# Two FFNs in fp32: four of eight k-tile pairs by seven products, two pairs with parts made by DMAs, and x accumulated in DRAM

## The chip, the core and the metric

The kernel runs on one core of a Trainium2 chip. The metric is the device time of the whole program in microseconds (us). Engines are named as the profile names them: PE is the matmul engine and PEld its weight loads, DVE the vector engine, ACT the scalar engine, POOL the GpSimd engine, SP the engine that issues most of the DMAs.

## The reference

The program is one fp32 forward pass of 256 tokens at width 2048 through two layers. Each layer is a mixer (a state-space scan beside sparse attention in the first; block attention beside a gated delta rule in the second) and an FFN with squared ReLU. The change concerns the two FFNs alone:

```python
# first layer, 256 tokens; w_up is 2048 x 8192, w_down 8192 x 2048
u = rmsnorm(x, g_mlp) @ w_up
return x + jnp.square(jax.nn.relu(u)) @ w_down
# second layer
return x + jnp.square(jax.nn.relu(h @ w_up)) @ w_down
```

## The kernel before

**Parts.** An fp32 value is split into a high part, the value rounded to the matmul format fp32r, and a low part, the value minus its high part. A product of fp32 operands is three matmuls: high by high, high of the activations by low of the weights, low of the activations by high of the weights (`product`, L250). Weights come from DRAM as fp32 in tiles `wst`, one SP DMA of 1024 KB each; ACT copies 1024 columns into a `whi` tile (L266) and DVE subtracts it into a `wlo` tile (L267). `stp` holds 3 tiles `wst`, `whp` and `wlp` 4 tiles each.

**A wide.** `wide` (L240) multiplies 256 tokens by a block of 2048 x 1024 weights. It goes through eight pairs j of two k-tiles (256 rows of weights) and accumulates in four of the eight PSUM banks at a time, and in four more for the parts of the seven products. For an ordinary pair each of two k-tiles meets two token tiles and two column halves: eight products, 24 matmuls of 128x512, in two ACT copies and two DVE subtractions. For j in `SPAIRS` = (2, 4, 6) the pair is treated as a 2 x 2 block product in seven products, 21 matmuls. DVE first makes four block differences of the weights (`t13` at L284, `t24` at L287 and L288), and the sums of the activation blocks stand ready in `forms[j]` (`two_forms`, `a_forms`). `shared` (L308) adds the PSUM banks together at the end, in four tiles of [128, 512].

**An FFN.** `ffn` (L374) has four stages `s_`, each with two wides of `w_up` and two of `w_down`; the last wide of `w_down` is done as two `panel`s instead. That makes 15 wides in one FFN and 30 in the program. I number them n = 0 to 14 in each FFN: n = 0, 1, 4, 5, 8, 9, 12, 13 are up wides and the rest down wides. Behind an up wide come squared ReLU (L382, L383) and 16 transposes on PE (L395), whose results are split into `hTh` and `hTl` (four k-tiles, two pairs, in each), and for pairs in `SPAIRS` are copied to `ff` (L399) and formed into `sfh` and `sfl`. Behind a down wide DVE adds the result to x, which lies in SBUF in four tiles X[p] of [128, 2, 512], in two additions for each quarter (L415, L418).

**Order and storage.** Each engine runs its instructions in the order that the tile scheduler has written down. Tiles come from pools with a fixed number of slots, and a tile waits for its slot until the last use of the tile that had it. The pool `sp` has 7 slots of 4 KB per partition. During an FFN four of these hold X, and the other three serve `t13` and `t24`. `ff` lies in the larger pool `s4`.

**POOL** has next to nothing to do: 51 rows in the program, among them the reciprocal roots of L159, and it issues no DMA in the FFNs.

Of the kernel before, what the change touches and what calls it, by code (L numbers as in the profile page):

```python
# [57 lines left out]
def build(ctx, tc, I, out, tap=None, upto=99):  # L58
    nc = tc.nc
# [179 lines left out]

    def wide(w, r0, c0, lhs, forms):  # L240

# [21 lines left out]
        def parts(src, n=1024):  # L263
            a = whp.tile([128, 1024], F32R, name="whi")
            b = wlp.tile([128, 1024], F32R, name="wlo")
            S.activation(a[:, :n], src, AF.Copy)  # L266
            V.tensor_tensor(b[:, :n], src, a[:, :n].bitcast(F32), op=OP.subtract)  # L267
            return [(a[:, o:o + 512], b[:, o:o + 512]) for o in range(0, n, 512)]

        for j in range(8):  # L270
            s = stp.tile([128, 2048], F32, name="wst")
            nc.sync.dma_start(s.rearrange("p (k n) -> p k n", k=2),
                              w[r0 + j * 256:r0 + j * 256 + 256, c0:c0 + 1024].rearrange("(k p) n -> p k n", p=128))
            if j not in SPAIRS:
                for kk in range(2):
                    xh, xl = lhs(2 * j + kk)
                    wl = parts(s[:, kk * 1024:(kk + 1) * 1024])[::-1]
                    for i, l, b in ((0, 0, "P2"), (0, 1, "P3"), (1, 0, "P4"), (1, 1, "E")):
                        h = slice(i * 128, i * 128 + 128)
                        product(b, xh[:, h], xl[:, h], *wl[l])  # L280
                continue
# [18 lines left out]
            product("P7", *sums(3), *u3)  # L300
            u2, u4 = parts(flat(t24))
            product("P6", *sums(2), *u2)
# [5 lines left out]
    def shared(B):  # L308

        p1, u2, u4, v = (s2([128, 512], name=n) for n in ("cp1", "cu2", "cu4", "cv"))  # L310
        S.activation(p1, B["P1"], AF.Copy)
        V.tensor_tensor(u2, B["P6"], p1, op=OP.add)
        V.tensor_tensor(u4, B["P5"], u2, op=OP.add)
        V.tensor_tensor(u2, B["P7"], u2, op=OP.add)
        V.tensor_tensor(v, B["P5"], u2, op=OP.add)
        return ((0, 0, p1, B["P2"]), (0, 1, u4, B["P3"]), (1, 0, u2, B["P4"]), (1, 1, v, B["E"]))

# [53 lines left out]
    def flat(ap):  # L371
        return ap.rearrange("p k c -> p (k c)")

    def ffn(X, act, forms, w_up, w_down, r, after, tail=0):  # L374
        for s_ in range(4):
            hT, hforms = [], {}
            for P in range(2):
                B, tags = wide(w_up, 0, s_ * 2048 + P * 1024, at_k(act), forms)
                us = {}
                for i, l, part, bank in shared(B):  # L380
                    V.tensor_tensor(part, bank, part, op=OP.add)
                    S.activation(part, part, AF.Relu, scale=r[:, i:i + 1])  # L382
                    S.activation(part, part, AF.Square)  # L383
                    us[i, l] = part
                for l in (1, 0):
# [3 lines left out]
                    for k0 in range(0, 4, 2):  # L389
# [11 lines left out]
                        else:  # L401
                            split(pt, flat(q[0][:, k0:k0 + 2]), flat(q[1][:, k0:k0 + 2]))
            for P in range(2):
                if (s_, P) == (3, 1):
                    for p in (2, 3):
# [4 lines left out]
                    continue  # L410
                B, _ = wide(w_down, s_ * 2048, P * 1024, at_k(hT), hforms)
                out_ = shared(B)
# [6 lines left out]
                if s_ == 3:  # L419
                    for p in range(2):  # L420
                        for t in range(2):
                            after(p, t)
# [367 lines left out]
    def add_panel(ps, p, scale, act, gain, ssx, forms):  # L790
# [601 lines left out]
```

## Time and profile before

| | us |
|---|---|
| three runs | 2635.05, 2633.22, 2637.54 |
| median | 2635.05 |
| the profiled execution, its own time | 2632.15 |
| its span | 2630.4 |
| first FFN in the trace, from its first to its last wide | 381.7 to 1102.6 |
| second FFN in the trace, with the end of the program | 1934.0 to 2621.6 |

The profiled execution is 2.9 us below the median, and its span leaves out 1.75 us at its ends. In the page, part 1 gives each engine's busy time as a share of the span, part 2 draws that over 40 slices of 66 us with the granted clock of PE, and part 6 gives the median time from issue to landing of each kind of DMA. A view by stretches gives busy times, the number of instructions in brackets, the granted clock, the DMA engines' mean share and the GB/s moved. A view of waits names who waits for whom, how long in total and how often. The timeline lists instructions by start and duration. PE's matmuls overlap each other, so the distance between two starts is what one of them takes of PE's time, and not its duration.

### The profile page before, as it was taken

What the parts mean: (1) busy time and instruction counts of PE and PEld (TensorE: products, weight loads), DVE (VectorE), ACT (ScalarE), POOL (GpSimd) and SP (SyncE); (2) the same over time, 40 slices, a digit from 0 to 9 for tenths busy, and PEclk for the clock granted to TensorE, in tenths of its full rate; (3) what the DMA queues carried; (4) which work ended last, traced back from release to release, by engine and by line L of the source; (5) the groups of instructions that cost most, each with busy time, mean ns of one, the idle gap of its engine ahead of it and who ended that gap; (6) DMA issues with size and microseconds to landing.
All of it is one profiled execution on the core that took longest, in us unless ns stands there. A gap on an engine that the chain in (4) does not pass through costs nothing.

```text
span 2630.4 us, 32664 instructions
## 1 busy us (share of the span) xinstructions
PE 2602.5 (99%) x12566; PEld 2171.2 (83%) x12566; DVE 2033.5 (77%) x2791; ACT 1463.4 (56%) x1956; POOL 38.6 (1%) x46
## 2 busy tenths in 40 slices
PE   8999999999999999999999999999999999999998
PEld 8998888878888888888888887888888888888886
DVE  5767768999989999676754767455579999999996
ACT  5455456646657566554533555444457566566664
POOL 0000000000000000000100000000000000000000
PEclk9999999999999999999999999999999999999999
DMA  7454555565555656653432743556555655565655
GB/s 239 142 176 157 168 192 192 179 205 192 192 201 183 208 194 199 210 186 119 133 96 87 252 166 112 180 189 211 198 180 178 215 199 195 193 207 191 208 179 173
DMA packets 192154, 478.64 MB, mean 182 GB/s; under 512 B 9127, under 2 KB 50046, under 8 KB 191998
## 3 DMA queue, kind: packets, MB, share of 16 engines
q1 hardware_dynamic: 185840, 467.57, 53.6%
q10 hardware_dynamic: 6158, 8.99, 1.0%
q8 instruction: 98, 1.61, 0.2%
q14 instruction: 58, 0.48, 0.1%
HBM read 472.32 MB, written 4.21 MB: 181 GB/s over the span
## 4 chain that ended last, share of the span: by engine, by line
PE 90%; DVE 5%; DMA 2%; ACT 1%; issue 1%; ACTq 0%; POOL 0%; POOLq 0%; SPq 0%; DVEq 0%
PE mm L255 21%; PE mm L193 13%; PE mm L194 13%; PE mm L192 13%; PE tp L255 10%; PE sx L255 9%; DVE wlo L267 3%; DMA wst<-in_w_down_dram 1%; PE sx L987 1%; PE sx L982 1%; PE tp L350 1%; ACT whi L266 1%; PE mm L395 1%; PE tp L881 0%; DVE wlo L208 0%
## 5 line engine op out<-in xcount | busy, mean ns | idle before, releaser
L208 DVE TENSOR_TENSOR wlo<-wst,whi 128x1024 fp32r<-128x1024 f32 (+6 forms) x416 | 475.7, 1146 | 319.8 <-ACT whi L207 316.8
L207 ACT ACTIVATE whi<-wst 128x1024 fp32r<-128x1024 f32 (+6 forms) x416 | 414.4, 998 | 461.7 <-PE mm L194 432.9
L266 ACT ACTIVATE whi<-wst 128x1024 fp32r<-128x1024 f32 x480 | 465.8, 979 | 275.8 <-PE mm L255 116.0
L267 DVE TENSOR_TENSOR wlo<-wst,whi 128x1024 fp32r<-128x1024 f32 x480 | 527.9, 1119 | 58.5 <-ACT whi L266 55.9
L266 ACT ACTIVATE whi<-t 128x1024 fp32r<-128x1024 f32 x180 | 190.2, 1057 | 214.2 <-DVE t L288 89.2
L193 PE MATMUL mm<-wlo,x2h 128*128 128x512 f32 (+3 forms) x736 | 279.1, 379 | 1.5 <-DVE wlo L208 1.5
L194 PE MATMUL mm<-whi,x2l 128*128 128x512 f32 (+3 forms) x736 | 279.2, 379 | 0.0
L192 PE MATMUL mm<-whi,x2h 128*128 128x512 f32 (+3 forms) x736 | 279.0, 379 | 0.0
L267 DVE TENSOR_TENSOR wlo<-t,whi 128x1024 fp32r<-128x1024 f32 x180 | 219.6, 1220 | 41.3 <-ACT whi L266 39.4
L193 PEld LDWEIGHTS mm<-wlo,x2h 128*128 128x128 f32 x736 | 138.9, 189 | 22.0 <-DVE wlo L208 2.1
L192 PEld LDWEIGHTS mm<-whi,x2h 128*128 128x128 f32 x736 | 138.9, 189 | 20.3 <-issue 1.1
L194 PEld LDWEIGHTS mm<-whi,x2l 128*128 128x128 f32 x736 | 138.6, 188 | 20.0 <-issue 0.9
L192 PE MATMUL mm<-whi,xnh 128*128 128x512 f32 (+3 forms) x416 | 152.6, 368 | 2.0 <-ACT whi L207 1.6
L255 PE MATMUL mm<-wlo,xnh 128*128 128x512 f32 x392 | 153.0, 390 | 0.0
L255 PE MATMUL mm<-whi,xnl 128*128 128x512 f32 x392 | 152.7, 390 | 0.0
L255 PE MATMUL mm<-whi,xnh 128*128 128x512 f32 x392 | 151.9, 391 | 0.7 <-ACT whi L266 0.7
L193 PE MATMUL mm<-wlo,xnh 128*128 128x512 f32 (+3 forms) x416 | 152.0, 366 | 0.0
L194 PE MATMUL mm<-whi,xnl 128*128 128x512 f32 (+3 forms) x416 | 150.7, 365 | 0.0
L255 PE MATMUL mm<-wlo,hTh 128*128 128x512 f32 x343 | 133.9, 390 | 0.0
L255 PE MATMUL mm<-whi,hTl 128*128 128x512 f32 x343 | 133.6, 389 | 0.0
L255 PE MATMUL mm<-whi,hTh 128*128 128x512 f32 x343 | 132.0, 390 | 0.0
L284 DVE TENSOR_TENSOR t<-wst 128x1024 f32<-128x1024 f32 x90 | 109.7, 1219 | 13.4 <-DMA wst<-in_w_down_dram 10.9
(531 smaller groups left out, 5407.9 us busy)
## 6 DMA issues: line engine op xcount, KB each, us to landing
wst<-in_w_up_dram SPq DMA_DIRECT2D x128, 1024.0 KB, 5.0
wst<-in_w_down_dram SPq DMA_DIRECT2D x128, 1024.0 KB, 5.4
wst<-in_w_in_dram SPq DMA_DIRECT2D x84, 1024.0 KB, 5.1
wst<-in_w_out_dram SPq DMA_DIRECT2D x16, 1024.0 KB, 5.1
wst<-in_w_o_dram SPq DMA_DIRECT2D x16, 1024.0 KB, 5.0
wst<-in_w_in_dram SPq DMA_DIRECT2D x16, 780.0 KB, 4.4
wst<-in_w_in_dram SPq DMA_DIRECT2D x12, 824.0 KB, 4.6
wst<-in_w_in_dram SPq DMA_DIRECT2D x12, 736.0 KB, 6.3
```

Of the source, the lines that this page charges most:

```text
L192: PE.matmul(ps[t][:, :n], xh[:, sl], wa, start=kt == first, stop=False)
L193: PE.matmul(ps[t][:, :n], xh[:, sl], wb, start=False, stop=False)
L194: PE.matmul(ps[t][:, :n], xl[:, sl], wa, start=False, stop=kt == last)
L207: S.activation(a[:, :2 * n], src, AF.Copy)
L208: V.tensor_tensor(b[:, :2 * n], src, a[:, :2 * n].bitcast(F32), op=OP.subtract)
L255: PE.matmul(B[b], x, y, start=left[b] == total[b], stop=left[b] == 1)
L266: S.activation(a[:, :n], src, AF.Copy)
L267: V.tensor_tensor(b[:, :n], src, a[:, :n].bitcast(F32), op=OP.subtract)
L284: V.tensor_tensor(t13, s.rearrange("p (k l n) -> p k l n", k=2, l=2)[:, :, 0], s[:, :1024].rearrange("p (l n) -> p l n", l=2)[:, ::-1], op ...
L350: PE.transpose(ps[:, kk, t, :], x[:, t, (k0 + kk) * 128:(k0 + kk + 1) * 128], ident)
L395: PE.transpose(pv[:, kk, t, :], us[t, l][:, c:c + 128], ident)
L982: PE.matmul(ps[:, i * 64:(i + 1) * 64].rearrange("p (m b) -> p m b", b=b), N[:, i], half(T[:, i], 0), start=True, stop=True)
```

## The change

- `SPAIRS` is (2, 3, 5, 6): four pairs of each wide go by seven products instead of three.
- Pair 4 of wides n = 0 to 13, and pair 0 of wides n = 1 to 13, are ordinary and their weights don't come through `wst`. `far_load` makes their parts: a GpSimd DMA of 512 KB from DRAM into an fp32r tile `fhi` rounds them; ACT writes the negative of `fhi` into `flo`; a second GpSimd DMA of the same weights is accumulated onto `flo`. That leaves `flo` = weights minus their high part. No DVE instruction is needed. Each pair takes four such DMAs, two rounding and two accumulating, so that 27 pairs make 108 DMAs in each FFN.
- Pair 4 of a wide is asked for when the code comes to pair 1 of the same wide, and pair 0 of the next wide when it comes to pair 5 (`hooks`).
- `fhi` and `flo` lie in the pool `sp`. X leaves it: x is stored to a DRAM tensor `xd` ahead of the FFN (ACT's queue), the results of the down wides of the first three stages are added to `xd` by accumulating GpSimd DMAs of 512 KB (12 in each FFN), and X is loaded again in the last stage. `ff` and the first of two result tiles, `ca`, move into `sp` too.
- `t24` is computed in place in `wst` and has no tile. The two additions of a down wide's result to X become one addition in the result tile (L467).
- An ordinary pair's products go to the banks P3, E, P2, P4 in this order.

Counted over the program, the order has 90 matmuls fewer (11950 rows of PE against 12040). The weights' SP DMAs in `wide` go from 240 to 186, the parts made by ACT and DVE from 660 to 612 each, `t13` from 90 to 120; ACT gets 108 negations and POOL 240 DMAs.

```diff
-    SPAIRS = (2, 4, 6)
+    SPAIRS = (2, 3, 5, 6)
...
-        f = s4([128, 2, 512], name="ff")
+        f = sp([128, 2, 512], name="ff")
...
+    def far_load(w, r0, c0, j):
+        parts = []
+        for kk in range(2):
+            src = w[r0 + (2 * j + kk) * 128:r0 + (2 * j + kk + 1) * 128, c0:c0 + 1024]
+            a, b = (sp([128, 1024], F32R, name=n) for n in ("fhi", "flo"))
+            G.dma_start(a, src)
+            S.activation(b, a.bitcast(F32), AF.Copy, scale=-1.0)
+            G.dma_start(b, src, accum_op=OP.add)
+            parts.append([(a[:, o:o + 512], b[:, o:o + 512]) for o in (0, 512)])
+        return parts
...
         for j in range(8):
+            if j in (hooks or {}):
+                hooks[j]()
+            if j in (far or {}):
+                for kk, wl in enumerate(far[j]):
+                    ordinary(j, kk, wl[::-1])
+                continue
             s = stp.tile([128, 2048], F32, name="wst")
...
-            t24 = sp([128, 2, 512], name="t24")
-            V.tensor_tensor(t24[:, 0], s[:, 1024:1536], t13[:, 0], op=OP.subtract)
-            V.tensor_tensor(t24[:, 1], s[:, 1536:], t24[:, 0], op=OP.subtract)
+            V.tensor_tensor(s[:, :512], s[:, 1024:1536], t13[:, 0], op=OP.subtract)
...
+            V.tensor_tensor(s[:, 1024:1536], s[:, 1536:], s[:, :512], op=OP.subtract)
...
-        p1, u2, u4, v = (s2([128, 512], name=n) for n in ("cp1", "cu2", "cu4", "cv"))
+        ca, cb = sp([128, 2, 512], name="ca"), s4([128, 2, 512], name="cb")
+        p1, u2, u4, v = ca[:, 0], ca[:, 1], cb[:, 0], cb[:, 1]
...
+            def mine():
+                far[4] = far_load(*todo[here], 4)
+
+            def following():
+                ready[here + 1] = far_load(*todo[here + 1], 0)
+            if here < 14:
+                hooks[1] = mine
+            if here < 13:
+                hooks[5] = following
...
+                if s_ == 3:
+                    for p in (2 * P, 2 * P + 1):
+                        X[p] = sp([128, 2, 512], name=f"X{p}")
+                        nc.scalar.dma_start(X[p], xd[:, p])
...
-                for i, l, part, bank in out_:
-                    x = X[2 * P + 1 - l][:, i]
-                    V.tensor_tensor(x, part, x, op=OP.add)
-                for i, l, part, bank in out_:
-                    x = X[2 * P + 1 - l][:, i]
-                    V.tensor_tensor(x, bank, x, op=OP.add)
...
+                    V.tensor_tensor(part, bank, part, op=OP.add)
...
+                    if s_ < 3:
+                        G.dma_start(xd[:, p], pair[l], accum_op=OP.add)
...
+        nc.scalar.dma_start(xd[:, p], X[p])
```

**Place 1, ACT and PE in the first down wide of the first FFN (n = 2), the order.** It stands directly behind an up wide, so that the transposes of that up wide (tiles `tp`, `sx`) are still being split while the down wide's first pairs run. ACT before, from the first of these evacuations:

```order
L399 ACTIVATE ff_4373<-tp_4368 128x512
L170 ACTIVATE hTh_4366<-sx_4385 128x512
L170 ACTIVATE hTh_4366<-ff_4373 128x512
L266 ACTIVATE whi_4511<-t13_4496 128x1024
L399 ACTIVATE ff_4399<-tp_4394 128x512
L170 ACTIVATE hTh_4392<-sx_4411 128x512
L170 ACTIVATE hTh_4392<-ff_4399 128x512
```

ACT after, at the same place:

```order
L170 ACTIVATE hTh_4408<-tp_4410 128x512
L448 ACTIVATE ff_4422<-sx_4417 128x512
L448 ACTIVATE ff_4441<-tp_4436 128x512
L170 ACTIVATE hTh_4408<-ff_4422 128x512
L170 ACTIVATE hTh_4434<-ff_4441 128x512
L170 ACTIVATE sfh_4430<-ff_4422 128x512
L170 ACTIVATE hTh_4434<-sx_4453 128x512
L247 ACTIVATE flo_4493<-fhi_4492 128x1024
L170 ACTIVATE sfh_4449<-ff_4441 128x512
L247 ACTIVATE flo_4498<-fhi_4497 128x1024
L281 ACTIVATE whi_4551<-t13_4538 128x1024
```

The negation that the accumulating DMA into `flo_4493` has to wait for stands behind seven evacuations on ACT.

PE before, at the end of pair 1 and the start of pair 2 of the same wide:

```order
L255 MATMUL mm1_4421<-whi_4478,hTh_3993 128x512
L255 MATMUL mm1_4421<-wlo_4479,hTh_3993 128x512
L255 MATMUL mm1_4421<-whi_4478,hTl_3994 128x512
L255 MATMUL tp_4422<-whi_4501,hTh_4009 128x512
L255 MATMUL tp_4422<-wlo_4502,hTh_4009 128x512
L255 MATMUL tp_4422<-whi_4501,hTl_4010 128x512
L255 MATMUL mm0_4419<-whi_4501,sfh_4024 128x512
```

PE after, at the same place:

```order
L267 MATMUL mm0_4461<-whi_4541,sfh_4052 128x512
L267 MATMUL mm0_4461<-wlo_4542,sfh_4052 128x512
L267 MATMUL mm0_4461<-whi_4541,sfl_4053 128x512
L267 MATMUL mm1_4463<-fhi_4492,hTh_4408 128x512
L267 MATMUL mm1_4463<-flo_4493,hTh_4408 128x512
L267 MATMUL mm1_4463<-fhi_4492,hTl_4409 128x512
L267 MATMUL mm1_4463<-fhi_4497,hTh_4408 128x512
L267 MATMUL tp_4465<-whi_4551,sfh_4052 128x512
```

Pair 4's parts (`fhi_4492`, `flo_4493`) are used inside pair 2, six matmuls after that pair began, where before pair 4 came behind pair 3. Between the fourth transpose into `tp_4410`, with which ACT's seven evacuations can begin, and the first matmul that reads `flo_4493`, the order of PE has 31 matmuls and 9 transposes.

**Place 2, POOL over three down wides and the up wide behind them.** In POOL's order of before these are all the rows of the same part of the program:

```order
L159 TENSOR_TENSOR rg_2946<-rv2_2944,mhalf_87 128x2
L159 TENSOR_TENSOR r2_3658<-rv2_3656,mhalf_87 128x2
L159 TENSOR_TENSOR r3_9351<-rv2_9349,mhalf_87 128x2
```

POOL after, from pair 4 of n = 2 (`fhi_4492`) on; `_4821` and `_4826` are pair 4 of n = 3, `ca` and `cb` the results of n = 2, `_4975` the next far pair:

```order
L246 DMA fhi_4492<-in_w_down_dram 128x1024
L246 DMA fhi_4497<-in_w_down_dram 128x1024
L248 DMA flo_4493<-in_w_down_dram 128x1024
L248 DMA flo_4498<-in_w_down_dram 128x1024
...
L248 DMA flo_4822<-in_w_down_dram 128x1024
L246 DMA fhi_4826<-in_w_down_dram 128x1024
L474 DMA xd_2971<-cb_4777 128x1024
L474 DMA xd_2971<-ca_4776 128x1024
L248 DMA flo_4827<-in_w_down_dram 128x1024
L246 DMA fhi_4975<-in_w_up_dram 128x1024
```

The additions to `xd` stand in one queue with the parts, and `fhi_4975` takes the slot of the result tile `ca_4776`, which comes free when its addition to `xd` has landed.

## Rows read from the trace of the kernel before

**Rows 1.** The page, part 1: busy time, share of the span, instructions.

```profile
PE 2602.5 (99%) x12566; PEld 2171.2 (83%) x12566; DVE 2033.5 (77%) x2791; ACT 1463.4 (56%) x1956; POOL 38.6 (1%) x46
```

**Rows 2.** The page, part 2: busy tenths in 40 slices, and PE's granted clock.

```profile
DVE  5767768999989999676754767455579999999996
PEclk9999999999999999999999999999999999999999
```

**Rows 3.** Stretches: length, PE, PEld, DVE, ACT, POOL busy (instructions), PEclk, DMA share, GB/s.

```profile
381.70:1102.60 720.90, 715.38 (x3220) 587.32 (x3219) 637.25 (x768) 436.63 (x534) 0.72 (x1) 1.00 0.59 195
1934.00:2621.60 687.60, 685.16 (x3077) 563.45 (x3075) 617.25 (x743) 418.89 (x504) 1.27 (x2) 1.00 0.56 193
447.50:490.60 43.10, 43.10 (x199) 35.56 (x198) 39.43 (x49) 29.66 (x37) 0.00 (x0) 1.00 0.60 194
490.60:532.50 41.90, 41.90 (x194) 34.55 (x193) 39.31 (x52) 28.84 (x38) 0.00 (x0) 1.00 0.56 179
```

**Rows 4.** Waits of PE from 400 to 1100 us: total, times, longest.

```profile
PE mm L192 <- DVE X L418: 2.6, 1, 2.6
PE tp L255 <- DVE wlo L267: 1.6, 3, 0.7
```

**Rows 5.** Timeline of PE in wide n = 2: start, duration, operation.

```profile
500.81 0.27 PE L395 MATMUL sx<-idt,cv 128*128 128x128 f32 x1
500.92 0.27 PE L395 MATMUL sx<-idt,cu 128*128 128x128 f32 x1
...
503.34 0.39 PE L255 MATMUL mm<-wlo,hTh 128*128 128x512 f32 x1
...
504.70 0.39 PE L255 MATMUL mm<-wlo,hTh 128*128 128x512 f32 x1
```

**Rows 6.** Timeline of ACT at the same place: start, duration, operation, idle before.

```profile
500.98 0.58 ACT L399 ACTIVATE ff<-tp 128x512 f32<-128x512 f32 x1
501.46 0.58 ACT L170 ACTIVATE hTh<-sx 128x512 fp32r<-128x512 f32 x1
501.94 0.62 ACT L170 ACTIVATE hTh<-ff 128x512 fp32r<-128x512 f32 x1
...
505.40 1.06 ACT L266 ACTIVATE whi<-t 128x1024 fp32r<-128x1024 f32 x1
507.06 0.63 ACT L170 ACTIVATE sfh<-ff 128x512 fp32r<-128x512 f32 x1 [0.60 <-DVE ff L235]
```

**Rows 7.** Groups of DVE by form: count, busy us, mean ns, idle before.

```profile
L267 DVE TENSOR_TENSOR wlo<-wst,whi 128x1024 fp32r<-128x1024 f32 x390 | 467.8, 1218 | 35.3 <-ACT whi L266 33.6
...
L284 DVE TENSOR_TENSOR t<-wst 128x1024 f32<-128x1024 f32 x90 | 109.7, 1219 | 13.4 <-DMA wst<-in_w_down_dram 10.9 <-DMA wst<-in_w_up_dram 1.9
...
L287 DVE TENSOR_TENSOR t<-wst,t 128x512 f32<-128x512 f32 x90 | 61.7, 685 | 0.6
...
L418 DVE TENSOR_TENSOR X<-mm,X 128x512 f32<-128x512 f32 x28 | 17.3, 680 | 0.0
```

**Rows 8.** Timeline of DVE in an up wide: start, duration, operation.

```profile
450.86 1.28 DVE L381 TENSOR_TENSOR cu<-mm,cu 128x512 f32<-128x512 f32 x2
...
452.65 2.35 DVE L267 TENSOR_TENSOR wlo<-wst,whi 128x1024 fp32r<-128x1024 f32 x2
```

**Rows 9.** DMA issues: queue, count, KB each, median us from issue to landing.

```profile
wst<-in_w_up_dram SPq DMA_DIRECT2D x128, 1024.0 KB, 5.0
...
X<-in_x_dram SPq DMA_DIRECT2D x4, 512.0 KB, 6.7
X<-in_x_dram ACTq DMA_DIRECT2D x4, 512.0 KB, 4.9
xsave<-X ACTq DMA_DIRECT2D x4, 512.0 KB, 5.4
X<-xsave ACTq DMA_DIRECT2D x4, 512.0 KB, 6.8
out_dram<-X SPq DMA_DIRECT2D x8, 256.0 KB, 2.7
...
C<-in_consts_dram SPq DMA_DIRECT2D x1, 832.0 KB, 8.6
```

**Rows 10.** Stretches at the program's start, columns as in the third group.

```profile
12.00:16.00 4.00, 4.00 (x21) 3.98 (x21) 2.32 (x4) 3.28 (x9) 0.00 (x0) 1.00 1.05 381
```

More of the change, by code (lines that the diff above doesn't have):

```diff
@@ L238, in a_forms, with wide @@
         forms[j] = sh, sl
-    def wide(w, r0, c0, lhs, forms):
+    def far_load(w, r0, c0, j):
[8 more added lines that the diff above has]
+        return parts
+    def wide(w, r0, c0, lhs, forms, far=None, hooks=None):
         ka, kb = (("mm0", "mm1"), ("tp", "sx"))[::1 - 2 * (turn[0] % 2)]
@@ L265, in parts, with ordinary @@
             b = wlp.tile([128, 1024], F32R, name="wlo")
-            S.activation(a[:, :n], src, AF.Copy)
-            V.tensor_tensor(b[:, :n], src, a[:, :n].bitcast(F32), op=OP.subtract)
-            return [(a[:, o:o + 512], b[:, o:o + 512]) for o in range(0, n, 512)]
-        for j in range(8):
+            av, bv = a[:, :n], b[:, :n]
+            if len(src.shape) == 3:
+                av, bv = (x.rearrange("p (l n) -> p l n", l=2) for x in (av, bv))
+            S.activation(av, src, AF.Copy)
+            V.tensor_tensor(bv, src, av.bitcast(F32), op=OP.subtract)
+            return [(a[:, o:o + 512], b[:, o:o + 512]) for o in range(0, n, 512)]
+        def ordinary(j, kk, wl):
+            xh, xl = lhs(2 * j + kk)
+            for i, l, b in ((0, 1, "P3"), (1, 1, "E"), (0, 0, "P2"), (1, 0, "P4")):
+                h = slice(i * 128, i * 128 + 128)
+                product(b, xh[:, h], xl[:, h], *wl[l])
+        for j in range(8):
+            if j in (hooks or {}):
[4 more added lines that the diff above has]
+                continue
             s = stp.tile([128, 2048], F32, name="wst")
@@ L275, in wide @@
                 for kk in range(2):
[L276 to L280, printed above, removed]
+                    ordinary(j, kk, parts(s[:, kk * 1024:(kk + 1) * 1024])[::-1])
                 continue
@@ L300, in wide @@
             product("P7", *sums(3), *u3)
-            u2, u4 = parts(flat(t24))
+            V.tensor_tensor(s[:, 1024:1536], s[:, 1536:], s[:, :512], op=OP.subtract)
+            u2, u4 = parts(s.rearrange("p (k l n) -> p k l n", k=2, l=2)[:, :, 0])
             product("P6", *sums(2), *u2)
@@ L372, in flat, with ffn, run @@
         return ap.rearrange("p k c -> p (k c)")
-    def ffn(X, act, forms, w_up, w_down, r, after, tail=0):
+    def ffn(act, forms, xd, w_up, w_down, r, after, tail=0):
+        todo = []
+        for s_ in range(4):
+            todo += [(w_up, 0, s_ * 2048 + P * 1024) for P in range(2)]
+            todo += [(w_down, s_ * 2048, P * 1024) for P in range(2)]
+        n = [0]
+        ready = {}
+        def run(lhs, forms):
+            here = n[0]
+            n[0] += 1
+            far = {}
+            if here in ready:
+                far[0] = ready[here]
+            hooks = {}
+            def mine():
[6 more added lines that the diff above has]
+                hooks[5] = following
+            return wide(*todo[here], lhs, forms, far, hooks)
         for s_ in range(4):
@@ L377, in ffn @@
             for P in range(2):
-                B, tags = wide(w_up, 0, s_ * 2048 + P * 1024, at_k(act), forms)
+                B, tags = run(at_k(act), forms)
                 us = {}
-                for i, l, part, bank in shared(B):
+                for i, l, part, bank in shared(B)[0]:
                     V.tensor_tensor(part, bank, part, op=OP.add)
@@ L410, in ffn @@
                     continue
-                B, _ = wide(w_down, s_ * 2048, P * 1024, at_k(hT), hforms)
-                out_ = shared(B)
+                B, _ = run(at_k(hT), hforms)
+                out_, pair = shared(B)
                 for i, l, part, bank in out_:
-                    x = X[2 * P + 1 - l][:, i]
-                    V.tensor_tensor(x, part, x, op=OP.add)
-                for i, l, part, bank in out_:
-                    x = X[2 * P + 1 - l][:, i]
-                    V.tensor_tensor(x, bank, x, op=OP.add)
-                if s_ == 3:
-                    for p in range(2):
+                    V.tensor_tensor(part, bank, part, op=OP.add)
+                    if s_ == 3:
+                        x = X[2 * P + 1 - l][:, i]
+                        V.tensor_tensor(x, part, x, op=OP.add)
+                for l in (1, 0):
+                    p = 2 * P + 1 - l
+                    if s_ < 3:
+                        G.dma_start(xd[:, p], pair[l], accum_op=OP.add)
+                    else:
                         for t in range(2):
@@ L797, in add_panel @@
             sumsq(ssx[:, t, p:p + 1], X[p][:, t])
+        nc.scalar.dma_start(xd[:, p], X[p])
+    xd = drp.tile([128, 4, 2, 512], F32, name="xd")
     X = x_panels()
@@ L818, in after1 @@
             nc.scalar.dma_start(xsave[:, p], X[p])
-    ffn(X, xn, xforms, I["w_up"][0], I["w_down"][0], r, after1)
+    ffn(xn, xforms, xd, I["w_up"][0], I["w_down"][0], r, after1)
     if upto == 2:
@@ L1329, in build @@
     xforms = {}
+    xd2 = drp.tile([128, 4, 2, 512], F32, name="xd2")
     ssx = tiny([128, 2, 4], "ssx", bufs=2)
@@ L1339, in build @@
             sumsq(ssx[:, t, p:p + 1], X[p][:, t])
+        nc.scalar.dma_start(xd2[:, p], X[p])
     r = x_rstd(ssx, "r4")
```

4 lines of the change are left out of this document (2 added, 2 removed).

## The prediction

> **What bounds the kernel now.** I read first the busy times of the page, then the stretches of the two FFNs, then the waits of PE, then the timeline at one place. PE is busy 99% of the span [rows 1], and its granted clock is full in every slice [rows 2], so a shorter time needs fewer matmuls, or the waits must grow for a longer one. The change touches the FFNs alone: PE is idle there for 720.90 - 715.38 = 5.5 us in the first and 2.4 us in the second [rows 3]. Those 7.9 us are all that removing waits could ever give. The waits named are short, the longest 2.6 us behind the additions to X at L418 [rows 4]. DVE comes next: 39.4 of 43.1 us in an up wide and 39.3 of 41.9 us in a down wide [rows 3]. ACT has 13 us free in each, POOL does nothing, and the DMA engines are busy 0.56 to 0.60 [rows 3]. So PE sets the time, and DVE would be first in the way of turning another pair into a seven.
>
> **What is removed.** 90 matmuls of 128x512. One takes (504.70 - 503.34) / 6 = 0.2267 us of PE [rows 5]. Term 1 is -90 x 0.2267 = -20.4 us, 0.8% of the time.
>
> **DVE.** Two subtractions in a row take 2.35 us against 1.22 for one [rows 7, 8], so each occupies 1.13; a 512-wide operation occupies about 0.60 (1.28 - 0.68 [rows 7, 8]). A seven costs DVE 1.13 + 2 x 0.6 + 3 x 1.13 + 0.6 = 6.3 us, and PE 21 x 0.2267 = 4.8. An ordinary pair costs DVE 2.3, and PE 24 x 0.2267 = 5.4. A far pair costs DVE nothing. An up wide goes from 3 x 6.3 + 5 x 2.3 to 4 x 6.3 + 2 x 2.3: 30.4 to 29.8, before the one `ff` more with its 1.2 us or so. Down wides lose four of eight additions to X, 2.4 us each. Over a wide DVE therefore stays inside PE, as now. But the sevens now stand in twos (2, 3 and 5, 6), each 1.5 us longer on DVE than on PE, with slack only from pairs beside them. ACT's 3.6 us of negations per wide lie in its 13 free us, and the loads of `wst` fall from eight to six.
>
> **The accumulating DMA behind an up wide (term 2).** This is where I expect the time. It concerns n = 1, 2, 5, 6, 9, 10, 13, so 14 wides. The order gives PE 31 matmuls and 9 transposes from the moment when ACT's evacuations can begin to the first use of `flo`: 31 x 0.2267 + 9 x 0.11 [rows 5] = 8.0 us. In that time ACT must do seven evacuations at 0.48 [rows 6], 3.4 us, up to 4.0 with a wait of 0.60 as the one for DVE there, then the negation, 1.06 long as a `whi` of the same size. From 8.0 that leaves 2.9 to 3.5 us, middle 3.2, for the DMA from issue to landing. All of PE's later work stands behind the matmul that waits for it, in order, and nothing is written there to fill in. The trace has no DMA from GpSimd, no rounding and no accumulation. The nearest rows are plain DMAs of 512 KB: 4.9, 5.4, 6.7 and 6.8 us [rows 9]. I take 5.9, the middle of 4.9 and 6.8. Below, a line through 256 KB (2.7) and 1024 KB (5.0) [rows 9] gives 2.7 + 2.3 / 3 = 3.5; above stands the 8.6 of the 832 KB row that landed among full queues at the start [rows 9]. Wait: 5.9 - 3.2 = 2.7 us, times 14 = +38 (0 by the lower end, 5.4 x 14 = 76 by the upper).
>
> By the Trainium skill, "DMA: Bandwidth & Descriptors", section on the anatomy of one DMA by the SWDGE (gpsimd) path, such a DMA takes about 2.0 us and its bytes at 436 GB/s. For 512 KB that is an estimate of 3.2 us, which would leave term 2 at nothing. The rows of the same size speak against it, since even the fastest is 4.9; no row here shows a GpSimd DMA.
>
> **The slot of `t13` (term 3).** With seven slots for `fhi`, `flo`, `t13`, `ff` and `ca`, the `t13` of pair 5 can begin only when pair 4's last matmul on an earlier slot is over. From there PE has about 14 matmuls, 3.2 us, to the first one on that `t13`, while DVE's `t13` and ACT's copy take 1.13 + 1.0, and DVE's subtraction 1.13 more: just enough where DVE is not behind. Two sevens in a row make DVE 2 x 1.5 = 3.1 us late against PE, less one 1.13 that the slack gives back, so between 0 and 2.0 us. I take 1.0 in each of the 14 wides, +14 (0 to 28).
>
> **`xd` in POOL's queue (term 4).** In n = 3, 4, 7, 8, 11 and 12 the next `fhi` stands behind the accumulations to `xd` of the same result tile and its slot. It must land, then ACT copies it, and ACT's next `whi` stands behind that copy. At 5.9 each for addition, rounding and accumulation the chain takes about 15 us with ACT's part, and the order gives PE about as much, 15.2 us of work, from release to use. I take 0.5 in each of 12 wides, +6 (0 to 3 x 12 = 36, were each DMA a microsecond longer).
>
> **What costs nothing.** The stores of x to `xd` and its reload: ACT issues them and is free 44% of the span [rows 1]; the reload is asked for a wide ahead of its use, some 40 us [rows 3] against 6.8 for a landing [rows 9]. Without that cover it would be 6.8 us at most, once per FFN. The matmuls' new order P3, E, P2, P4 doesn't change their number. Of the waits of now, L418's 2.6 us go; that is within the 7.9 us.
>
> **Sum.** -20.4 + 38 + 14 + 6 = +37.6. The profiled execution took 2632.15 us, so 2669.7; the median of the runs lies 2.9 above it, so **2673 us** is forecast. By the rows of 512 KB alone (4.9 to 6.8, with terms 3 and 4 from zero to 28 and 12) it goes from 2639 to 2705.
>
> **Rivals.**
> 1. *The DMA is short.* If an accumulation lands in 3.5 us or less, PE never waits for it, DVE gets its early start, and the saved matmuls stay saved: 2635 - 20.4 = 2615, up to 4 us more by 0.3 us of wait in 14 wides: 2615 to 2619. Its place is the first `flo` of n = 1, 2 and so on, and it decides at about 3.5 us per DMA. For it: the line through 256 and 1024 KB, and DMA engines that are free 40% of the time. Against it: every 512 KB row, and that an accumulation has also to read what it adds to. It is also the time that the skill's formula would give. Chance 0.25.
> 2. *The waits and the matmuls cancel.* At about 4.4 us per DMA term 2 is 17 us and the others a few: within 5 us of now, 2637. Chance 0.07.
> 3. *The DMA engines fill.* A wide moves 8 MB now at a share of 0.6 [rows 3]. After, it is six loads of 1 MB, four roundings and four accumulations of 0.5 MB, so 10 MB, or 12 with the target read again and up to 13 with x: 0.75 to 0.97 of full, since 0.6 goes with 8 MB. The rate at full share was 381 GB/s [rows 10]. Then 8.6 us for each DMA is the nearest row, and the terms are 76 + 28 + 36 - 20 = +120: 2755. It decides when the share in an FFN goes above about 0.9. Against it: the loads of 1 MB still landed in 5.0 at 0.6. Chance 0.18.
>
> That the change doesn't do what it says I leave out: the matmuls of the order are exactly 90 fewer.
>
> **Chances.** The forecast has 0.50, on the slower side, the rivals 0.25, 0.07 and 0.18. A change under 0.2%, about 5 us, can't be told from none here. Faster by more: 0.25; within: 0.07; slower by more: 0.68. The range of 8 in 10 takes in rival 1 from 2613, the 2 us below for a part of the 7.9 us, and the forecast with the middle of the way to rival 3, 2725; beyond lies most of rival 3 and little else. The likeliest case's own range is 2639 to 2705.
>
> **What would show it.** Right: PE waits at the line of the ordinary products for a DMA into `flo`, about 14 times and 2 to 3 us each, `flo` landing in 5 to 7 us, and PE's busy time about 20 us less. DVE would show slack, and 512 KB from GpSimd a share of the DMA engines near 0.75. Wrong: `flo` landing within 3.5 us, with PE still at 99%; or waits of PE for `t13` and `whi` that are longer than those for `flo`, which would make term 3 the large one; or waits in n = 3, 4, 7, 8, 11, 12, which would make term 4 so. A granted clock that falls where PE waits is not in the sum, since no row here is below full clock, and would add to it.

## The result: 7% slower

The changed kernel takes 2820.73 us (2815.96 to 2828.6, four runs) against 2635.61 us before: 1.0713 times as long, interval 1.07 to 1.0726, or 185 us more. The forecast of 2673 had the direction and not the size; the range ended at 2725. The profiled execution took 2820.39 us, 188 us more than that of before.

Part 1 of the page after, and the two queues that carry the weights, from part 3 (packets, MB, share of 16 engines):

```profile
PE 2669.3 (95%) x12476; PEld 2162.7 (77%) x12476; DVE 2024.1 (72%) x2833; ACT 1500.7 (53%) x2036; POOL 214.6 (8%) x286
...
q1 hardware_dynamic: 171152, 410.95, 43.4%
q0 software_dynamic: 34560, 125.84, 20.3%
```

PE has exactly 90 matmuls fewer than in [rows 1], and is nevertheless busy 67 us longer (the forecast had about 20 us less), and idle 121 us longer. Four wides of the first FFN, n = 1, 2, 3 and 4, as stretches (columns as in [rows 3]; a wide is taken from one copy of P1, L334, to the next):

```profile
447.90:499.70 51.80, 47.01 (x198) 37.04 (x198) 41.08 (x55) 32.16 (x42) 5.72 (x8) 0.93 0.73 204
499.70:549.10 49.40, 44.51 (x197) 34.75 (x196) 40.68 (x55) 31.82 (x41) 6.26 (x9) 1.00 0.79 222
549.10:599.80 50.70, 45.01 (x183) 34.86 (x183) 36.45 (x42) 22.42 (x25) 7.48 (x10) 0.97 0.87 238
599.80:645.90 46.10, 42.94 (x181) 33.17 (x181) 34.58 (x39) 22.32 (x25) 6.92 (x9) 1.00 0.86 235
```

The same four took 43.5, 44.0, 42.5 and 42.0 us before. The loss lies in every wide, also in n = 3 and 4, where the forecast had half a microsecond. No engine is full: DVE is busy 35 to 41 of 46 to 52 us. What ends PE's waits, over the whole program (total, times, longest):

```profile
PE mm L267 <- DVE wlo L282: 18.5, 33, 1.6
PE mm L267 <- ACT whi L281: 17.5, 25, 2.3
PE tp L267 <- DVE wlo L282: 15.0, 19, 1.6
PE sx L267 <- DMA flo<-in_w_up_dram: 14.9, 6, 3.3
PE mm L267 <- DMA flo<-in_w_up_dram: 14.6, 5, 3.2
...
PE mm L267 <- DMA flo<-in_w_down_dram: 9.4, 5, 2.6
PE sx L267 <- DMA flo<-in_w_down_dram: 8.0, 5, 2.5
```

The waits for `flo` are there as forecast: 46.9 us in 21 waits. By the timeline 19 of them lie in the 14 wides that the forecast named, 42.9 us or 3.1 us per wide where it had 2.7; the other two, of 2.1 and 1.9 us, are in n = 0. But the waits for `whi` and `wlo`, parts of the sevens, are larger together (72.7 us in all six rows for them, of which the three largest are shown), and they had almost no term. In the first FFN they come to 24.9 us in the six wides n = 3, 4, 7, 8, 11 and 12, about 4 us each, against about 2 in the others.

**A wait can also cost clock.** Timeline of PE in n = 1 (start, duration), and the granted clock of the stretch behind the wait:

```profile
471.25 0.39 PE L267 MATMUL sx<-fhi,xnh 128*128 128x512 f32 x1
474.73 0.80 PE L267 MATMUL sx<-flo,xnh 128*128 128x512 f32 x1 [3.09 <-DMA flo<-in_w_up_dram]
475.32 0.63 PE L267 MATMUL sx<-fhi,xnl 128*128 128x512 f32 x1
475.75 0.63 PE L267 MATMUL sx<-fhi,xnh 128*128 128x512 f32 x1
...
481.13 0.39 PE L267 MATMUL mm<-whi,sfl 128*128 128x512 f32 x1
481.36 0.40 PE L267 MATMUL sx<-wlo,xnh 128*128 128x512 f32 x1
```

```profile
474.10:480.90 6.80, 6.17 (x15) 4.82 (x16) 5.43 (x7) 4.39 (x5) 0.00 (x0) 0.50 0.81 203
```

After 3.09 us of waiting the granted clock is 0.50, the lower of its two levels, for 6.8 us, and matmuls start 0.43 us apart in place of 0.23. The 15 matmuls in it cost 15 x 0.2 = 3 us more, as much as the wait itself. The clock doesn't fall each time. In n = 9 it stays full behind 3.21 us:

```profile
868.39 0.50 PE L267 MATMUL sx<-flo,xnh 128*128 128x512 f32 x1 [3.21 <-DMA flo<-in_w_up_dram]
```

```profile
868.40:874.90 6.50, 6.33 (x27) 4.92 (x28) 5.91 (x8) 4.43 (x5) 0.86 (x2) 1.00 0.73 198
```

Of the eight waits for `flo` above 2 us in the first FFN, five have matmuls at the lower clock behind them, and three (2.41, 2.62 and 3.21 us) have none. So these runs don't show what decides it. The page's 40 slices of the clock show 9 throughout, before and after, and hide all of this.

### The profile page after: what moved, and what is told of

It is laid out like the page before. It is cut to its first block, busy times and chain, and to the rows that moved or that the text cites. A ratio compares the mean times of both kernels' runs of the same rounds, so it can differ in the third digit from the quotient of the medians.

```text
span 2818.6 us, 33160 instructions
## 1 busy us (share of the span) xinstructions
PE 2669.3 (95%) x12476; PEld 2162.7 (77%) x12476; DVE 2024.1 (72%) x2833; ACT 1500.7 (53%) x2036; POOL 214.6 (8%) x286
## 3 DMA queue, kind: packets, MB, share of 16 engines
q0 software_dynamic: 34560, 125.84, 20.3%
## 4 chain that ended last, share of the span: by engine, by line
PE 61%; issue 20%; DVE 7%; DMA 6%; ACT 3%; POOL 2%; ACTq 0%; POOLq 0%; DVEq 0%; SPq 0%
PE mm L193 12%; PE mm L194 12%; PE mm L192 12%; PE mm L267 9%; PE tp L267 4%; PE sx L267 4%; DVE wlo L282 3%; DMA xd<-ca 1%; ACT whi L281 1%; DMA flo<-in_w_up_dram 1%; DMA flo<-in_w_down_dram 1%; DVE t L307 1%; POOL fhi L246 1%; POOL flo L248 1%; PE sx L1044 1%
## 5 line engine op out<-in xcount | busy, mean ns | idle before, releaser
L282 DVE TENSOR_TENSOR wlo<-wst,whi 128x1024 fp32r<-128x1024 f32 (+1 forms) x492 | 515.1, 1090 | 127.3 <-ACT whi L281 127.0
L281 ACT ACTIVATE whi<-wst 128x1024 fp32r<-128x1024 f32 (+1 forms) x492 | 437.1, 945 | 235.8 <-DVE wst L322 139.0
L247 ACT ACTIVATE flo<-fhi 128x1024 fp32r<-128x1024 f32 x108 | 113.9, 1055 | 282.3 <-DMA fhi<-in_w_up_dram 100.6
L282 DVE TENSOR_TENSOR wlo<-t,whi 128x1024 fp32r<-128x1024 f32 x120 | 146.5, 1221 | 71.5 <-ACT whi L281 71.2
L281 ACT ACTIVATE whi<-t 128x1024 fp32r<-128x1024 f32 x120 | 126.0, 1050 | 33.7 <-DVE t L307 20.1
L267 PE MATMUL mm<-wlo,sfh 128*128 128x512 f32 x240 | 102.9, 429 | 18.7 <-DVE wlo L282 18.5
L267 PE MATMUL mm<-whi,sfh 128*128 128x512 f32 x240 | 98.2, 425 | 17.6 <-ACT whi L281 17.5
L267 PE MATMUL mm<-whi,sfl 128*128 128x512 f32 x240 | 97.8, 407 | 0.0
L246 POOL DMA_DIRECT2D fhi<-in_w_up_dram x60 | 39.0, 649 | 700.7 <-DVE sfl L172 401.8
L267 PE MATMUL mm<-wlo,xnh 128*128 128x512 f32 x232 | 91.7, 395 | 0.0
```

The lines of the kernel that those rows point to most:

```text
L246: G.dma_start(a, src)
L247: S.activation(b, a.bitcast(F32), AF.Copy, scale=-1.0)
L267: PE.matmul(B[b], x, y, start=left[b] == total[b], stop=left[b] == 1)
L281: S.activation(av, src, AF.Copy)
L282: V.tensor_tensor(bv, src, av.bitcast(F32), op=OP.subtract)
```

## Experiments

The experiments make a ladder from the kernel before to the changed one. Medians where an interval is given, otherwise one execution; the kernel before took 2632 to 2636 us beside them. The four runs of one kernel lie 2 to 13 us apart, so a step of some 10 us that rests on a single execution is weak.

| kernel | us | step |
|---|---|---|
| before | 2635 | |
| x in DRAM, old pools (e15) | 2666 | +31 |
| and `ff`, result tile in `sp` (e8) | 2695 | +29 |
| and a fourth seven (e5) | 2703 | +8 |
| and `t24` in place (e1) | 2741 | +38 |
| and far pairs of two rounding DMAs each (e3) | 2732 | -9 |
| and negation and accumulation: the changed kernel | 2821 | +89 |

The steps depend on their order: a cost that is plain in one kernel can be hidden in another. The fourth seven, for one, stands here ahead of the far pairs that were to free DVE for it. I tell the runs from the bottom of the ladder, as they were made.

**The far pairs left out (e1).**

```diff
-            if here < 14:
-                hooks[1] = mine
-            if here < 13:
-                hooks[5] = following
```

> The changed kernel with the far pairs taken out: pairs 0 and 4 get their parts from wst by ACT and DVE as the other ordinary pairs; four sevens, x in DRAM and t24 in place stay. Theory A (the far pairs cost the time: ACT's negation waits in ACT's queue for the rounding DMA and holds back the copies whi behind it): those waits go, what is left is 20 us less of matmuls and DVE's larger load, 44 us against PE's 42 in an up wide, so 16 x 2.2 = 35 us back: about 2650. Rival R1 (seven slots in sp hold up t13): also about 2650, since four slots come free. Rival R2 (two sevens in a row make DVE late, whatever the far pairs do): PE keeps waiting for whi and wlo, over 2720.

2741.47 us, ratio 1.0408 (1.039 to 1.0425). The far pairs cost 80 us, net of the work of ACT and DVE that their pairs take again here, and 106 us are there without them. My theory A, that they are the whole cost, fell.

**The accumulating DMA left out (e2), and negation and accumulation replaced by a second rounding DMA (e3).**

```diff
 # e2
-            G.dma_start(b, src, accum_op=OP.add)
 # e3
-            S.activation(b, a.bitcast(F32), AF.Copy, scale=-1.0)
-            G.dma_start(b, src, accum_op=OP.add)
+            G.dma_start(b, src)
```

> The changed kernel without the accumulating DMA into flo, so that flo is only the negative of the high part: the far pairs' true low parts are left out. Negation and rounding DMA stay. Theory A: PE's waits for flo go (about 3.3 us in 14 wides, 46 us, and 10 to 15 us of half clock), the waits for whi and wlo, about 100 us, stay: 2750 to 2770. Rival R3 (the accumulation is the whole cost): 2640 or less.

> The changed kernel with flo loaded by a second rounding DMA in place of negation and accumulation: the far pairs' true low parts are left out. The DMAs' number and bytes stay the same, but for the reading of flo; ACT has no instruction of the far pairs. Theory A: waits for whi go and flo is early: 2620 to 2660. R1 (slots): t13 still waits for the slots of far pairs, 2700 or more. R2 (two sevens in a row): 2720 or more. R4 (the DMA engines are too full): 2750 or more.

2774.96 and 2731.95 us. The accumulation is worth 2821 - 2775 = 46 us in this kernel. That is not term 2 of the forecast (38) alone: the waits for `flo` go, and so do half of the DMAs of the far pairs, POOL's queue falling from 20.3% to 9.4% of the engines. From e2 to e3 the negation leaves ACT and one more DMA for each tile comes in, and 43 us go. So the negation's place costs about as much as the accumulation. ACT in the changed kernel (waits over the whole program, then the timeline in n = 8):

```profile
ACT flo L247 <- DMA fhi<-in_w_up_dram: 100.6, 23, 9.4
ACT flo L247 <- DMA fhi<-in_w_down_dram: 80.7, 12, 10.1
```

```profile
802.78 1.06 ACT L281 ACTIVATE whi<-wst 128x1024 fp32r<-128x1024 f32 x1 [1.64 <-DMA wst<-in_w_up_dram]
812.71 1.06 ACT L247 ACTIVATE flo<-fhi 128x1024 fp32r<-128x1024 f32 x1 [8.86 <-DMA fhi<-in_w_up_dram]
813.67 1.05 ACT L281 ACTIVATE whi<-t 128x1024 fp32r<-128x1024 f32 x1
```

ACT runs in order. It stands 8.86 us at the negation until `fhi` has landed, and the copy `whi` of a seven, whose `t13` had long been ready, stands behind it. The part `wlo` made from that copy then reaches PE late:

```profile
816.03 0.50 PE L267 MATMUL tp<-wlo,sfh 128*128 128x512 f32 x1 [0.63 <-DVE wlo L282]
```

Of ACT's 8.86 us about 1.2 come out on PE at this place, as this wait and the two behind it (0.34 and 0.25 us).

But e3, with no instruction of the far pairs on ACT or DVE, is still 97 us slower than before, and its matmuls are 90 fewer. The accumulation and the queue on ACT explain 89 us and no more. The wides of e3 say where the rest is (n = 1, then n = 3):

```profile
442.10:491.30 49.20, 45.06 (x196) 34.07 (x195) 41.08 (x55) 27.89 (x38) 4.21 (x8) 1.00 0.63 210
538.30:580.50 42.20, 42.00 (x184) 33.81 (x182) 35.40 (x41) 19.01 (x22) 6.10 (x10) 1.00 0.91 280
```

n = 3 is as short as before (42.5 us), while n = 1 and n = 2, with 49.2 and 47.0 us, are not.

**The sevens apart (e4).**

```diff
-    SPAIRS = (2, 3, 5, 6)
+    SPAIRS = (1, 3, 5, 7)
```

> The changed kernel with the sevens at pairs 1, 3, 5, 7 in place of 2, 3, 5, 6, each behind a far or an ordinary pair. R2 (two sevens in a row make DVE late): the waits for whi and wlo halve, 2760 or less. Theory A and R1: within 25 us of the changed kernel, 2795 to 2845, since negations and slots stay.

2911.87 us, outside what any theory gave. PE's waits for `whi` there are 158.5 us in the two largest rows, the longest 6.6:

```profile
PE mm L267 <- ACT whi L281: 80.4, 16, 6.6
PE tp L267 <- ACT whi L281: 78.1, 16, 6.6
```

Part of them is the same queue on ACT: the one of 3.91 us at 575.01 follows a negation that waited 10.00 us for its `fhi`. The one of 6.59 us at 524.87 follows the evacuations of the transposes and two negations that waited for no DMA. The clock over the program is 0.957 too, against 0.984. So taking the sevens apart doesn't mend the changed kernel, but the run doesn't tell what two in a row cost.

**`t24` in a tile of its own: without far pairs (e5), and in the changed kernel (e7).**

```diff
-            V.tensor_tensor(s[:, :512], s[:, 1024:1536], t13[:, 0], op=OP.subtract)
+            t24 = sp([128, 2, 512], name="t24")      # e7: s4
+            V.tensor_tensor(t24[:, 0], s[:, 1024:1536], t13[:, 0], op=OP.subtract)
+            V.tensor_tensor(t24[:, 1], s[:, 1536:], t24[:, 0], op=OP.subtract)
...
-            V.tensor_tensor(s[:, 1024:1536], s[:, 1536:], s[:, :512], op=OP.subtract)
```

> e1_no_far with t24 in a tile of its own, both halves made right behind t13 as in the kernel before, in place of the second half made in wst behind the first parts. Theory B (t24 in place: its second half can only be written when ACT and DVE have read the block that it overwrites, so the copy whi behind it and the products behind that are late): PE's waits behind L322 go, what is left is DVE's 45 us in a wide behind an up wide against 43.5 to 44 of before, 16 x 1.5 = 24 us: 2645 to 2665. Rival R2 (two sevens in a row, with their DVE load): 2715 to 2745.

> The changed kernel, far pairs and all, with t24 in a tile of its own (from the pool s4). Theory B and A together: the gain of e5_no_far_own_t24 over e1_no_far comes here too, 70 to 95 us: 2725 to 2750, and what is left over the kernel before is the far pairs' cost, 90 to 115 us. If the far pairs' waits alone set the time in the changed kernel, the in-place half is hidden beneath them: 2800 or more.

2703.08 us (1.0261, 1.0243 to 1.0278) against 2741 in place, and 2811.99 against 2821. In place, the second half of `t24` (L322) overwrites a block that ACT and DVE must have read first. ACT then has to wait for L322, and PE for ACT (e1, n = 2, ACT, then PE):

```profile
524.12 2.53 ACT L281 ACTIVATE whi<-wst 128x1024 fp32r<-128x1024 f32 x3 [3.03 <-DVE wst L322]
```

```profile
525.23 0.50 PE L267 MATMUL sx<-whi,sfh 128*128 128x512 f32 x1 [0.58 <-ACT whi L281]
```

Without the far pairs that is worth 38 us. With them it is 9, perhaps since the same matmuls are late anyway, which no run shows (and `t24` comes from `sp` in e5, from `s4` in e7): theory B's 70 to 95 us came in neither kernel. In e5 the wides behind an up wide are still slow, and there DVE is nearly full, as the theory said, 45 of 47.5 us, where before it was 40.3 of 44:

```profile
486.60:534.10 47.50, 45.09 (x198) 34.56 (x198) 44.97 (x59) 31.96 (x42) 0.00 (x0) 1.00 0.52 177
```

**x in DRAM without the fourth seven: `t24` in place (e6), in its own tile (e8).** Both are e1 and e5 with `SPAIRS` (2, 4, 6).

> e1_no_far with the three sevens of the kernel before, pairs 2, 4 and 6: x in DRAM, t24 in place and the new order of an ordinary pair's products are the only changes to the kernel before. Theory B: PE waits behind the in-place half here too, 90 sevens at 0.5 to 1.5 us: 2670 to 2750. R2: no two sevens are neighbours and DVE has no more to do than before: 2625 to 2645.

> e6_x_in_dram_alone with t24 in its own tile: against the kernel before only x moves to DRAM and an ordinary pair's products come in another order. Theory B (the in-place half of t24 is what e6 lost): the 58 us of e6 go, and DVE has 2.4 us less in a down wide: 2625 to 2640. Rival (x's additions in DRAM and its reload cost time): 2665 or more. The difference to e5_no_far_own_t24 (2703) is then the fourth seven with its DVE work: 65 to 75 us net, with 20 us of matmuls saved in it.

2692.7 us and 2695.41 us (1.0235, 1.0218 to 1.0252). Theory B fell here: with three sevens apart the in-place half costs nothing. And 60 us come with x in DRAM and the moved tiles alone, for which the forecast had nothing. From e8 to e5 the fourth seven is +8, its 20 us of matmuls in it; with `t24` in place, from e6 to e1, it is +49. So the in-place half costs only together with a fourth seven.

**The fourth seven only where DVE is free (e9).**

```diff
+            return wide(*todo[here], lhs, forms, far, hooks, SPAIRS if here % 4 in (0, 3) else (2, 4, 6))
```

> e8_x_in_dram_own_t24 with a fourth seven, pair 0, only in the 14 wides that stand behind a down wide (n = 0, 3, 4, 7, 8, 11, 12 of each FFN), where DVE was busy 39.8 of 42.6 us in e1; the wides behind an up wide keep sevens 2, 4, 6. Theory (DVE's load in the wides behind an up wide is what a fourth seven loses): 14 x 3 x 0.2267 = 9.5 us less than e8: 2615 to 2630. Rival (any fourth seven makes DVE late): e8 plus 10 to 30 us.

2700.09 us (1.0251, 1.0236 to 1.0266), 5 us more than e8, with overlapping intervals: no gain of it reached the end, though 42 matmuls are gone, and the theory that DVE's load behind an up wide is what a fourth seven loses fell with it.

**The pool `sp`: `ff` back in `s4` in the changed kernel (e10).**

> The changed kernel with ff back in the pool s4, so that the seven slots of sp serve fhi, flo, t13 and ca alone. R1 (slots of sp): t13 and the far pairs start earlier, DVE's 66 us of waits for PE at t13 fall by half and the time to 2790 or less. If the slots are not what holds t13 and fhi up, within 15 us of the changed kernel: 2805 to 2835.

2807.73 us, 13 less; R1 had 2790 or less. But PE's waits changed altogether. Those for `flo` are gone but for 1.7 us, with every accumulation still there, and those for `whi` and `wlo` have grown from 72.7 to 103.5 us:

```profile
PE mm L267 <- ACT whi L281: 27.2, 40, 2.3
...
PE mm L267 <- DMA flo<-in_w_down_dram: 1.7, 3, 0.7
```

The slots are why `flo` was late. In n = 1 of the changed kernel the first `fhi` of pair 4 waits for one, and its `flo` is issued 21.3 us behind the wide's start at 447.93 (first two lines, POOL). In e10 that `flo` is issued 5.7 us behind the start at 442.22 (last line):

```profile
460.76 0.56 POOL L246 DMA_DIRECT2D fhi<-in_w_up_dram  x1 [20.73 <-PE tp L267]
469.18 0.89 POOL L248 DMA_DIRECT2D flo<-in_w_up_dram  x1 [5.32 <-ACT flo L247]
```

```profile
447.95 0.86 POOL L248 DMA_DIRECT2D flo<-in_w_up_dram  x1 [10.08 <-ACT flo L247]
```

So R1 holds for the waits for `flo`, and little of it for the time: without those 45 us of waits the sevens' parts hold PE up instead.

**The additions to x left out: of e8 (e11), of the changed kernel (e12).**

```diff
                     if s_ < 3:
-                        G.dma_start(xd[:, p], pair[l], accum_op=OP.add)
```

> e8_x_in_dram_own_t24 without the 24 accumulating DMAs into xd (the down wides' results of three stages are left out of x). Theory C (each pair of additions to xd shares the DMA engines with a load of wst, which takes 8.2 us in place of 5.1; DVE, in order at that load's t13, waits 4 us, and PE 2 to 3): the 12 wides behind such a pair lose their 2 to 2.5 us each, 25 to 30 us: 2660 to 2670. What then is left over the kernel before, 25 to 35 us, is the order of the work. Rival (the order alone, the late loads are hidden): 2685 to 2697.

> The changed kernel without the 24 accumulating DMAs into xd (the down wides' results of three stages are left out of x). Theory C: the wides behind them lose the chain of addition, slot of ca, rounding DMA, negation and whi as well: 12 wides at 3 to 5 us, 2760 to 2785. Rival (far pairs wait for their own DMAs there anyway): 2800 or more.

2656.84 and 2796.06 us: 39 and 25 us less. The mechanism is seen in e8. In the stretch from 545 to 546 us the queues are (packets, MB, share of 16 engines), with the load of `wst` issued in it, and under it a load issued 5 us earlier, from the stretch from 540 to 541 us:

```profile
q0 software_dynamic: 39, 0.16, 98.9%
q1 hardware_dynamic: 5, 0.01, 2.2%
...
wst<-in_w_down_dram SPq DMA_DIRECT2D x1, 1024.0 KB, 8.6
```

```profile
wst<-in_w_down_dram SPq DMA_DIRECT2D x1, 1024.0 KB, 5.5
```

The additions take nearly all of the DMA engines' time from there to 549 us (90% or more in each stretch of 1 us), and the load beside them lands 3 us later. DVE in e8 then stands, in order, at the `t13` of that load:

```profile
549.25 0.68 DVE L311 TENSOR_TENSOR t<-wst,t 128x512 f32<-128x512 f32 x1
553.92 1.23 DVE L307 TENSOR_TENSOR t<-wst 128x1024 f32<-128x1024 f32 x1 [4.00 <-DMA wst<-in_w_down_dram]
```

Without the additions (e11) the wides behind a down wide take less than before, n = 4 for one, where DVE is busy 36.1 us against 38.3 before:

```profile
574.70:616.20 41.50, 41.50 (x184) 34.22 (x183) 36.10 (x39) 22.30 (x23) 0.00 (x0) 1.00 0.59 203
```

**The order of an ordinary pair's products: in the kernel before (e13), and the old order in e8 (e14).**

> The kernel before with an ordinary pair's products in the changed order P3, E, P2, P4, and no other change. The first parts of the next wide meet other banks first, which the end of the wide before may still hold. Theory D (the order moves the scheduler's placing and costs some of what e8 lost): 2640 to 2660. Rival: nothing, 2630 to 2640.

> e8_x_in_dram_own_t24 with the products and the banks' additions in the order of the kernel before, P2, P3, P4, E. Theory C: the additions to xd still collide, 2660 or more. Theory D: 2640 to 2660.

2635.24 us, ratio 1.0003 (0.9994 to 1.0013): the order alone is nothing. In e8 the old order makes 2719.72 us, 24 more; I have no reading of why.

**The old pools for `ff` and the result tiles, x in DRAM (e15); the additions spread (e16).**

```diff
+        f = s4([128, 2, 512], name="ff")
...
+        p1, u2, u4, v = (s2([128, 512], name=n) for n in ("cp1", "cu2", "cu4", "cv"))
...
 # e15: the result lies in four tiles, so its additions to xd are four of 256 KB
+                            G.dma_start(xd[:, p, i], pair[l][i], accum_op=OP.add)
 # e16: the four 256 KB additions are queued, one hook each
+            for j in (1, 3, 5, 7):
+                hooks[j] = one
```

> e8_x_in_dram_own_t24 with the forms ff back in the pool s4 and the result tiles of a wide back in four tiles of the pool s2, so that x in DRAM (added by four accumulating DMAs of 256 KB) and the order of an ordinary pair's products are all that differs from the kernel before. Theory E (ff and ca in sp made t13 wait for their slots behind an up wide: e11 is 22 us slower than before with no addition to x at all): these 20 us go, 2655 to 2680, and what stays is the collision of the additions with the loads. Rival (the pools make no difference): 2685 to 2700.

> e15_x_in_dram_old_pools with the four additions of 256 KB held back and issued one by one at pairs 1, 3, 5 and 7 of the next wide. Theory C: a load of wst that shares the DMA engines with 256 KB in place of 1 MB is late by under 1 us, and DVE saves 2.4 us in each down wide: 2620 to 2636, no slower than the kernel before. Rival (an accumulation delays the load beside it whatever its size): 2650 or more.

2666.09 us and 2666.54 us (1.0128, 1.0111 to 1.0145). With the old pools the wides behind an up wide are as before, and those behind an addition are long, with n = 14. n = 2 and n = 3 of e15:

```profile
484.20:528.20 44.00, 44.00 (x202) 36.12 (x201) 40.14 (x53) 30.42 (x40) 0.00 (x0) 1.00 0.59 191
528.20:573.90 45.70, 43.14 (x182) 34.75 (x182) 36.65 (x41) 22.30 (x24) 3.76 (x4) 0.96 0.69 208
```

In e8 n = 2 took 46.8 us. So the tiles that moved into `sp` are worth about 29 us, the size of the additions, which differs too, included, and the additions about the rest. e16 doesn't test its theory: in its trace the four additions still leave POOL one behind the other, within 2 us, and the last three wait for nothing. Whether smaller or later additions would slip past the loads stays open. No kernel here beats the one before.

## Why the forecast was wrong, step by step

Two steps failed: term 4, which priced the wait on ACT at 0.5 us in 12 wides, and "What costs nothing", which put the additions to `xd` and the moved and reused tiles at nothing or nearly so. Three signs that the prediction names for being wrong came: waits for `whi` longer than those for `flo`, waits in n = 3, 4, 7, 8, 11 and 12, and a clock that falls.

- **The matmuls saved (-20.4):** right, 12566 to 12476.
- **The accumulating DMA (+38):** right in the place and the length of the waits, 3.1 us where it had 2.7. What they cost is less sure: 46 us by e2, which takes DMA load away as well, and 13 by e10, which ends nearly all of them by a slot for `ff` elsewhere. The term took the late negation as given by ACT's order and left out the wait of `fhi` for its slot. The landing was sized rightly: `flo` lands in 5.6 and 6.1 us (median, up and down), where the sum had 5.9 from the rows of 512 KB in [rows 9]:

```profile
fhi<-in_w_up_dram POOLq DMA_DIRECT2D x60, 512.0 KB, 5.1
flo<-in_w_up_dram POOLq DMA_DIRECT2D x60, 512.0 KB, 5.6
fhi<-in_w_down_dram POOLq DMA_DIRECT2D x48, 512.0 KB, 6.5
flo<-in_w_down_dram POOLq DMA_DIRECT2D x48, 512.0 KB, 6.1
...
xd<-cb POOLq DMA_DIRECT2D x12, 512.0 KB, 8.3
xd<-ca POOLq DMA_DIRECT2D x12, 512.0 KB, 10.2
```

  The estimate of 3.2 us by the Trainium skill's formula ("DMA: Bandwidth & Descriptors", the anatomy of one SWDGE DMA) is under all of them; the nearest is a rounding DMA in e2, 4.0 to 4.1 us. Rival 1 was rightly the less likely.
- **Slots (+14):** no run measures the term by itself. e10 moves only `ff` and gains 13 us, and the slots delayed `fhi`, where the term had them delay `t13`.
- **POOL's queue (+6):** far too small. Term 4 named the copy `whi` that stands behind ACT's copy of `fhi`, but took the chain as covered by 15.2 us of PE's work but for 0.5 us. ACT's negation waits up to 10 us for `fhi` with the copies of sevens behind it; its place on ACT is 43 us by e2 and e3, one execution each. In these wides PE waits about 4 us for sevens' parts. The term also took 5.9 us for an addition to `xd`, and these land in 8.3 and 10.2.
- **"What costs nothing":** the step that failed most. x in DRAM was judged by its stores and its reload; the additions were costed only as a place in POOL's queue, and not as load on the DMA engines beside a load of `wst` that DVE needs at once. That is 39 us in e8 and 25 in the changed kernel. The moved tiles (29 us between e15 and e8) had only their place in term 3's list of slots, and the in-place half of `t24` (38 or 9) had no term at all.
- **DVE by sums:** 30 us of work per wide before and after, and DVE is indeed less busy now, by 9 us over the program. But the sum of a wide doesn't tell whether a chain `t13`, copy, subtraction comes in time. Without far pairs the fourth seven's saving of 20 us ended as a loss of 8 (e5 against e8), with DVE at 45 us there; how it fares with DVE relieved and `t24` in its own tile, no run separates.
- **The clock:** named as outside the sum, and not small. Over the FFNs the granted clock is 0.97 and 0.98 of full, so an estimate from these lines is 741.3 x 0.03 + 724.2 x 0.02 = 37 us of the 185, shared out among the costs above:

```profile
400.00:1141.30 741.30, 677.11 (x2836) 526.47 (x2835) 578.60 (x718) 412.85 (x509) 87.99 (x120) 0.97 0.77 217
2024.00:2748.20 724.20, 668.69 (x2839) 518.44 (x2838) 577.92 (x718) 412.43 (x509) 88.01 (x120) 0.98 0.77 223
```

- **Rival 3** had the DMA engines at 0.75 to 0.97 with its effect from 0.9 on. The share is 0.77 on average and 0.87 and 0.86 in n = 3 and 4: the average was right and the wrong thing to ask. In e3, n = 3 takes 42.2 us at 0.91, so a high share alone doesn't slow a wide, while in e8 a burst of 1 MB fills the engines for some 4 us in a wide whose share is 0.70.

What stays open: the cost of each step in the changed kernel itself, where they hide one another (e7, e10 and e12 together give 47 us, if they add); why e14 is slower than e8; what decides whether the clock falls behind a wait; and the 2.6 us of n = 14 in e15.

## What to carry to other kernels

When PE is busy 99% and every other engine is in order behind it, a step that is moved must be costed by what is queued behind its wait on its own engine, and by whom its DMAs meet at that moment, not by its own duration or by averages over a stage. An edit that only moves a tile to another pool or reuses a buffer in place can add waits as one that adds work does, so it wants a line in the sum. A wait that is removed is not time that is won, where the next one stands close behind it (e10). And a PE wait of 2 or 3 us can cost up to about twice its length, because the clock was the lower one behind five of the eight looked at here.

## Not expected of the hardware

An accumulating DMA takes the DMA engines 1.7 to 1.9 times as long as one without, by the time that a queue's packets took. The 24 additions of e8 put 12.58 MB through POOL's queue in 2.6% of 2688.2 us, 0.18 MB per us of all engines, where the loads on the other queue make 467.57 MB in 51.2%, 0.34. For the far pairs the same 125.84 MB of POOL's queue take 15.8% of 2730.2 us, 431 us, with two rounding DMAs each (e3), and 20.3% of 2818.6 us, 572 us, when one of the two accumulates. Rounding alone, with the additions to x taken off, makes (125.84 - 12.58) / (431 - 70) = 0.31 MB per us, close to a plain load.
